# Head of a batch-norm matmul: one more small early read of x, wider early reads of w, eight small idle matmuls fewer

## The chip, the cores and the metric

The kernel runs on one core of one Trainium2 chip. The metric is the device time of one execution in microseconds (us). One execution was also recorded by the hardware profiler; its times are counted from the start of the span, that is from the first recorded instruction.

## The reference

`x` has 16 x 512 rows of 1024 values, `weight` (called w below) is 1024 x 768, both float32. Taken as one matrix, x has 8192 rows.

```
y = np.matmul(x, weight)
mean = np.mean(y, axis=(0, 1), keepdims=True)
var = np.var(y, axis=(0, 1), keepdims=True)
y_norm = (y - mean) / np.sqrt(var + eps)
return (gamma * y_norm + beta).astype(np.float32)
```

The mean and the variance of a column go over all 8192 rows, so nothing of a column can be written out before the whole column has been multiplied.

## The kernel before

**Tiling.** The rows of x are worked off in 16 chunks of 512 rows (`CH`). The 768 columns are six blocks of 128. In the first stage PE multiplies as x arrives: `rows_unit` (matmuls of line 493) makes column blocks 0 and 1 with rows on the partitions, and `col_unit` (matmuls of line 558) makes the other blocks with columns on the partitions, for the first chunks while x still arrives, for the others in later passes over x, which stays in SBUF. ACT and DVE take the results out of PSUM and collect sums; in the later stages the results are normalised, turned and stored. The last column block has an end of its own.

**Loading.** All loads of x and w are issued by POOL's queue and turn float32 into bf16 on the way. `load_x` (line 392) issues four transfers for each stretch of rows, one for each quarter of the 1024 columns. `load_w` (line 383) issues four transfers, one for each quarter `i` of w's 1024 rows. A quarter of w has four blocks of 64 rows, numbered by `jw`; two neighbouring rows are one 1536-value run on a partition. The first entries of the list of loads are

```
order = [("x", 0), ("w", 0, 2), ("x", 1), ("w", 2, 4)]
```

that is: x's first 256 rows (called x0 here), the blocks jw = 0 and 1 of every quarter (w's first pair), x's next 256 rows (x1), the blocks jw = 2 and 3 (w's second pair). Each is four transfers. A queue has eight completion slots, so a ninth transfer waits for the first one's landing, and so on.

**Turning x.** DVE transposes x's loaded rows into `xT_sb` (lines 414 and 421), for the first chunk in two halves per 256 rows.

**Order of work.** Tasks with a cost, dependencies and a due time go to a planner (`arrange`), which fixes one order of instructions per engine; `seq` chains the instructions of an engine in this order. The code around the change, the instructions ahead of the planner's first task, is written out by hand and is not planned.

**The head.** While the first loads are under way, three things happen that compute nothing of the result:

- `wake` (lines 574 and 577) runs idle matmuls on a cleared tile: `WAKE` = 8 with 512 float32 columns (each takes two passes in the profile), then `SMALL` = 16 small ones with 128 bf16 columns.
- `touched` (lines 342 to 345) is a small tile that nobody reads. SP issues four transfers into it, one for each quarter of w. Each reads a single 4-byte value out of every second row of block jw = 0, 32 values.
- a second call of `wake` (`FILL` = 1, one large idle matmul, two passes) stands between the first chunk's two halves.

After the first `wake`, PE's order is: eight matmuls of line 493 and sixteen of line 558 on x0 and w's first pair, the filling idle matmul, the same 24 matmuls on x1 and w's first pair, then the first chunk's matmuls with w's second pair.

Of the kernel before, what the change touches and what calls it, by code (L numbers as in the profile page):

```python
# [227 lines left out]
def kernel(  # L228
# [9 lines left out]
    nc = tc.nc  # L238
    f32 = mybir.dt.float32
# [8 lines left out]
    P = 128  # L248
# [5 lines left out]
    QR = 256  # L254
    QPC = CH // QR
    JW = KQ // 64
    PIECES = ((0,QR),(QR,QR))
    WAKE = 8
    FILL = 1
    SMALL = 16  # L260
    TOUCH = 1
    EARLY = 4
    SHORT = 2
# [16 lines left out]
    x_flat = x.flatten_outer_dims()  # L280
    out_flat = out.flatten_outer_dims()

    singles = ctx.enter_context(tc.tile_pool(name="singles", bufs=1))
# [7 lines left out]
    def seq(bi):  # L291

        ins = bi.ins
        prev = last.get(ins.engine)
        if prev is not None:
            tc.add_manual_dep(
                ins, prev,
                mybir.DependencyInfo(mybir.DependencyClass.NoSync, mybir.DependencyReason.DATA),
                reason="order",
            )  # L300
        last[ins.engine] = ins.name
        return bi
# [36 lines left out]
    warm = singles.tile([P, 1], f32)  # L339

    seq(nc.scalar.activation(warm, eps_sb, AF.Sqrt))
    touched = singles.tile([P, TOUCH], f32)
    first_rows = weight.rearrange("(i jw c e) n -> i jw c (e n)", i=4, jw=JW, e=2)
    for i in range(4):
        seq(nc.sync.dma_start(touched[32 * i:32 * i + 32], first_rows[i, 0, :, 0:TOUCH]))


    tasks, turns = [], {}
# [83 lines left out]
    t = 1.0  # L432
    affine = None
    for kind, n, *n1 in order:
# [21 lines left out]
        for i in range(rows // QR):  # L456
            c, q = divmod(m0 // QR + i, QPC)
# [9 lines left out]
        if rows % QR:  # L467
            t0 = rows // QR * QR // 32
            m1 = m0 + 32 * t0
            c, q = divmod(m1 // QR, QPC)  # L470
# [99 lines left out]
    def wake(count, slot):  # L570
        def emit(eng):
# [3 lines left out]
            small = idle_sb[:, 0:P // 2].bitcast(bf16)  # L575
            for _ in range(SMALL if count == WAKE else 0):
                seq(nc.tensor.matmul(idle_ps[:, 0:P], small, small, start=True, stop=True))
# [361 lines left out]
    k = 0  # L939
# [330 lines left out]
    for c, r0, rows in ends:  # L1270
        due = E + 2.0 + 0.6 * c
        n = max(rows // CH, 1)
# [70 lines left out]
```

## Time and profile before

| | |
|---|---|
| median of 3 runs | 207.59 us (207.12 to 207.87) |
| the profiled execution's own time | 207.45 us |
| its span, first to last instruction | 205.6 us |
| PE busy | 190.8 us, 93% of the span |
| DVE busy | 157.4 us, 77% |
| ACT busy | 139.9 us, 68% |
| POOL busy | 129.3 us, 63% |
| HBM read and written | 36.71 MB and 25.17 MB |

The 1.85 us between the profiled execution's time and its span lie ahead of the first and behind the last recorded instruction. A row of the timeline or of the chain gives the start and the length in us, then the engine, the line and the tiles; `x8` says that eight instructions are merged into it. "issue" in the chain is time in which an engine waits for nothing that the profile shows. In a table by windows, PEclk is the granted TensorE clock as a share of full speed, "DMA share" the packets' time as a share of the time of 16 DMA engines (above 1 where packets overlap), and GB/s what was moved, counted in bytes as written.

### The profile page before, as it was taken

The page shows a single profiled execution, that of the slowest core. Times are in us where ns is not written, and L with a number is a line of the kernel's source. Part 1 is how long each engine was busy: PE and PEld are TensorE (multiplying, and loading weights), DVE is VectorE, ACT ScalarE, POOL GpSimd, SP SyncE. Part 2 cuts the span into 40 slices and gives each one's busy share as a digit, 9 for nine tenths or more (in the row PEclk, how much of TensorE's full clock was granted, in tenths as well). Part 3 has the DMA queues.
Part 4 walks back from the last instruction along what each step waited for, and adds up shares of the span by engine and source line. Part 5 has one row for each costly group of instructions (what it writes and reads, how often), then busy time and mean ns, then how long its engine had stood idle before and what let it go on. Part 6 is the DMA issues. An engine that isn't in the chain of part 4 may idle for free.

```text
span 205.6 us, 3501 instructions
## 1 busy us (share of the span) xinstructions
PE 190.8 (93%) x1211; PEld 118.0 (57%) x1226; DVE 157.4 (77%) x239; ACT 139.9 (68%) x248; POOL 129.3 (63%) x143
## 2 busy tenths in 40 slices
PE   7999999999999999999999999999999999996900
PEld 3467565656588888777865444444444445553900
DVE  4202979989999999969989998888999648947900
ACT  2000461468989999998879777997376776875960
POOL 7766964787399979997304998599945440440000
PEclk9999999999999999999999999999999999999695
DMA  5999999999999999999696898999999999999898
GB/s 60 151 200 198 194 196 196 199 195 196 190 193 196 197 196 196 196 197 195 101 143 205 312 338 286 260 354 312 318 323 217 324 311 324 270 344 346 247 347 254
DMA packets 98433, 48.73 MB, mean 237 GB/s; under 512 B 24176, under 2 KB 97904, under 8 KB 98416
## 3 DMA queue, kind: packets, MB, share of 16 engines
q0 software_dynamic: 34624, 18.36, 65.2%
q1 hardware_dynamic: 63792, 30.16, 53.2%
q8 instruction: 9, 0.15, 0.3%
q14 instruction: 8, 0.07, 0.1%
HBM read 36.71 MB, written 25.17 MB: 301 GB/s over the span
## 4 chain that ended last, share of the span: by engine, by line
PE 86%; DMA 3%; ACT 3%; POOL 2%; issue 1%; DVE 1%; ACTq 0%; POOLq 0%
PE y_ps L558 53%; PE y_ps L493 24%; PE y_ps L797 4%; DMA w_sb<-in_weight_dram 3%; ACT o_sb L1292 3%; PE o_ps L1027 2%; POOL ring L392 1%; PE a_ps L886 1%; PE y_ps L736 1%; POOL w_sb L383 1%; PE o_ps L1057 0%; ACTq L1338 0%; PE idle_ps L574 0%; PE tot_ps L854 0%; DVE fin L743 0%
## 5 line engine op out<-in xcount | busy, mean ns | idle before, releaser
L558 PEld LDWEIGHTS <-w_sb 128*128 128x128 bf16 x520 | 50.4, 97 | 56.9
L558 PE MATMUL y_ps<-x_pl,w_sb 128*128 128x512 bf16 x256 | 60.5, 379 | 0.3
L392 POOL DMA_DIRECT2D ring<-in_x_dram x76 | 47.5, 629 | 14.2 <-DVE xT_sb L414 5.0
L558 PE MATMUL y_ps<-xT_sb,w_sb 128*128 128x512 bf16 (+1 forms) x249 | 55.0, 370 | 0.4
L493 PE MATMUL y_ps<-w_sb,xT_sb 128*128 128x256 bf16 x448 | 50.4, 273 | 0.6 <-DMA w_sb<-in_weight_dram 0.5
L493 PEld LDWEIGHTS <-xT_sb 128*128 128x128 bf16 x448 | 43.6, 98 | 8.0 <-issue 1.0
L421 DVE STREAM_TRANSPOSE xT_sb<-ring 128x1024 f32<-128x1024 f32 (+1 forms) x29 | 31.2, 1112 | 14.1 <-DMA ring<-in_x_dram 13.9
L694 DVE BATCH_NORM_STATS2 stats<-y_ps 128x6 f32<-128x512 f32 x46 | 30.8, 687 | 12.0 <-PE y_ps L558 11.8
L698 ACT CAST y_sb<-y_ps 128x512 bf16<-128x512 f32 x51 | 29.4, 590 | 13.3 <-DVE stats L694 11.3
L925 POOL TENSOR_TENSOR ring<-ring,sum 128x1024 f32<-128x1024 f32 (+1 forms) x11 | 23.8, 2192 | 14.6 <-DVE ring L920 14.6
L642 ACT ACTIVATE sq_sb<-y_ps 128x512 f32<-128x512 f32 x28 | 16.3, 610 | 17.9 <-PE y_ps L493 17.7
L649 POOL TENSOR_TENSOR sum<-sum,sq_sb 128x512 f32<-128x512 f32 x20 | 25.6, 1280 | 3.5 <-ACT sq_sb L642 2.7
L530 ACT COPY x_pl<-xT_sb 128x1024 bf16<-128x1024 bf16 x24 | 24.4, 1057 | 1.7 <-DVE xT_sb L421 1.7
L645 DVE TENSOR_TENSOR sum<-y_ps,sum 128x512 f32<-128x512 f32 x28 | 18.9, 675 | 6.3 <-ACT sq_sb L642 5.3
L655 ACT CAST y_sb<-y_ps 128x512 bf16<-128x512 f32 x28 | 16.1, 598 | 7.9 <-DVE sum L645 7.7
L530 POOL COPY x_pl<-xT_sb 128x1024 bf16<-128x1024 bf16 x15 | 16.4, 1128 | 7.7 <-DVE x_pl L530 4.9
L920 DVE TENSOR_TENSOR ring<-y_sb,a_ps 128x1024 f32<-128x1024 bf16 (+1 forms) x16 | 16.7, 1080 | 0.8 <-DMA out_dram<-ring 0.8
L1192 ACT CAST ring<-ring 128x1024 f32<-128x1024 bf16 x15 | 15.7, 1049 | 1.6 <-DMA ring<-y_sb 1.6
L1027 PE MATMUL o_ps<-ident,y_sb 128*128 128x128 bf16 x104 | 14.5, 248 | 2.2 <-DVE y_sb L1279 2.0
L1138 POOL TENSOR_TENSOR ring<-ring,sum 128x1024 f32<-128x1024 f32 x4 | 9.7, 2414 | 10.9 <-DVE ring L1134 10.9
L414 DVE STREAM_TRANSPOSE xT_sb<-ring 128x2048 bf16<-128x2048 bf16 x6 | 13.5, 2289 | 0.3 <-DMA ring<-in_x_dram 0.2
L574 PE MATMUL idle_ps<-idle_sb 128*128 128x512 f32 x18 | 10.7, 749 | 1.5 <-DVE idle_sb L314 1.5
(97 smaller groups left out, 155.1 us busy)
## 6 DMA issues: line engine op xcount, KB each, us to landing
out_dram<-ring SPq DMA_DIRECT2D x38, 512.0 KB, 3.8
ring<-in_x_dram POOLq DMA_DIRECT2D x52, 256.0 KB, 8.8
out_dram<-o_sb SPq DMA_DIRECT2D x6, 512.0 KB, 4.4
ring<-in_x_dram POOLq DMA_DIRECT2D x16, 128.0 KB, 6.0
w_sb<-in_weight_dram POOLq DMA_DIRECT2D x8, 192.0 KB, 6.2
out_dram<-ring SPq DMA_DIRECT2D x4, 256.0 KB, 3.1
ring<-in_x_dram POOLq DMA_DIRECT2D x4, 192.0 KB, 8.0
out_dram<-o_sb SPq DMA_DIRECT2D x3, 256.0 KB, 2.5
```

Of the source, the lines that this page charges most:

```text
L392: bi = seq(nc.gpsimd.dma_start(x_bf[32 * i:32 * i + 32], src[:, :, KQ * i:KQ * (i + 1)]))
L421: seq(nc.vector.transpose(dst, src[:, :, jw0:jw1]))
L493: seq(nc.tensor.matmul(y_ps[:, s], x_of(c, jw, e, t * P, (t + 1) * P), w_sb[:, jw, e, 0:NA], start=(s == 0 and jw == 0 and e == 0), stop=( ...
L530: seq(nc.scalar.copy(dst, pairs) if eng == "ACT" else ENG[eng].tensor_copy(dst, pairs))
L558: seq(nc.tensor.matmul(y_ps, w_sb[:, jw, e, nt * P:(nt + 1) * P], moving(c, jw, e, q0 * QR, q1 * QR, parted), start=(jw == 0 and e == 0 an ...
L645: seq(nc.vector.tensor_add(sum1, slot.tile[:, 0:n], sum1))
L649: seq(ENG[eng].tensor_add(acc, acc, state["sq"][:, 0:n]))
L694: seq(nc.vector.bn_stats(dst, slot.tile))
L698: seq(nc.scalar.copy(y(nt, c), slot.tile))
L920: seq(nc.vector.tensor_mul(slot.o, y_row[c].y[:, s0:s1], aff[0][:, None, :].to_broadcast([P, n, NA])))
L925: seq(ENG[eng].tensor_add(slot.o, slot.o, row[:, None, :].to_broadcast([P, n, NA])))
L1027: seq(nc.tensor.transpose(dst, src, ident))
```

## The change

Three edits, all at the head. The number of small idle matmuls goes from 16 to 8. SP issues one more small transfer, ahead of the others: one 4-byte value of each of x's first 256 rows. The four transfers on w read twice as many values, from blocks jw = 0 and jw = 1 instead of jw = 0 alone.

```
-    SMALL = 16
+    SMALL = 8
...
-    touched = singles.tile([P, TOUCH], f32)
-    first_rows = weight.rearrange("(i jw c e) n -> i jw c (e n)", i=4, jw=JW, e=2)
+    touched = singles.tile([P, 4, TOUCH], f32)
+    first_x = x_flat[0:QR].rearrange("(t p) k -> p t k", p=P)
+    seq(nc.sync.dma_start(touched[:, 2:4], first_x[:, :, 0:TOUCH]))
+    first_rows = weight.rearrange("(i jw c e) n -> i c jw (e n)", i=4, jw=JW, e=2)
     for i in range(4):
-        seq(nc.sync.dma_start(touched[32 * i:32 * i + 32], first_rows[i, 0, :, 0:TOUCH]))
+        seq(nc.sync.dma_start(touched[32 * i:32 * i + 32, 0:2], first_rows[i, :, 0:2, 0:TOUCH]))
```

The order of instructions on the other engines stays. PE has 16 rows fewer (eight matmuls and their weight loads), SP has one transfer more, ahead of the four.

## Prediction

> **What bounds the kernel now.** I read the chain that ended last first, because the change is all at the head and the chain tells whether the head reaches the end.
>
> ```profile
> PE 86%; DMA 3%; ACT 3%; POOL 2%; issue 1%; DVE 1%; ACTq 0%; POOLq 0%
> ```
>
> Then the same chain in order of time, its first pieces:
>
> ```profile
> 1.29 2.44 POOL ring L392 x4
> 3.74 1.21 POOL w_sb L383 x3
> 4.95 0.36 issue
> 5.31 7.09 DMA w_sb<-in_weight_dram
> 12.40 0.14 issue
> 12.53 1.03 PE y_ps L493 x8
> 13.57 1.81 PE y_ps L558 x16
> 15.38 0.86 PE idle_ps L574 x2
> 16.24 0.87 PE y_ps L493 x8
> 17.11 1.81 PE y_ps L558 x16
> 18.93 0.07 issue
> ```
>
> The only DMA in the chain is the fourth transfer of w's first pair, issued at 5.31 and landed at 12.40. From 12.53 to 187.96 the chain holds nothing but PE and issue pieces of about 0.05. So PE begins when w's first pair has landed, and whatever that landing gains is kept to the end, unless a later arrival takes its place. Next the timeline around that point, to see what PE does before it and what follows close behind:
>
> ```profile
> 10.96 1.06 PE L577 MATMUL idle_ps<-idle_sb 128*128 128x128 bf16 x16
> ...
> 12.53 1.03 PE L493 MATMUL y_ps<-w_sb,xT_sb 128*128 128x256 bf16 x8 [0.51 <-DMA w_sb<-in_weight_dram]
> ...
> 15.24 1.30 DVE L421 STREAM_TRANSPOSE xT_sb<-ring 128x512 f32<-128x512 f32 x2 [5.16 <-DMA ring<-in_x_dram]
> ```
>
> The idle matmuls end at 10.96 + 1.06 = 12.02, and PE then stands for 0.51 us. Last, the table by windows: how fast do the first transfers run?
>
> ```profile
> 3.50:4.50 1.00, 1.00 (x3) 0.48 (x2) 0.00 (x0) 0.00 (x0) 1.00 (x3) 1.00 1.21 149
> 4.50:5.50 1.00, 1.00 (x2) 0.39 (x2) 0.00 (x0) 0.00 (x0) 1.00 (x3) 1.00 1.19 150
> 5.50:6.50 1.00, 1.00 (x2) 0.34 (x1) 0.00 (x0) 0.00 (x0) 1.00 (x3) 1.00 1.43 125
> 6.50:7.50 1.00, 1.00 (x3) 0.38 (x2) 0.00 (x0) 0.30 (x1) 0.89 (x3) 1.00 0.92 100
> 7.50:8.50 1.00, 1.00 (x4) 0.49 (x3) 0.00 (x0) 0.00 (x0) 0.57 (x1) 1.00 0.92 136
> 8.50:9.50 1.00, 1.00 (x4) 0.46 (x3) 0.72 (x2) 0.00 (x0) 0.57 (x2) 1.00 1.11 212
> ```
>
> The last column is GB/s. From 8.5 to 18.5 the ten windows of 1 us give 212, 206, 194, 185, 193, 211, 221, 206, 207 and 182, mean 202. The five from 3.5 to 8.5 fall short of that by 1 - 149/202 and so on: 0.26 + 0.26 + 0.38 + 0.50 + 0.33 = **1.73 us of stream time lost**, 0.52 of it while only x0 flows, 1.21 where x0 ends and w begins. The same kinds of transfers for x1 and w's second pair, from 12 on, show no such dip.
>
> **The change part by part.**
>
> *Eight small idle matmuls fewer.* Sixteen start within 15/16 of 1.06 - 0.22 = 0.84 us (0.219 is one's duration), 0.056 apart, so eight fewer end 8 x 0.056 = 0.45 earlier, at 11.57. By themselves they bring nothing: PE then waits 0.96 instead of 0.51 for the same landing. They only set how early PE can take an earlier landing: 12.53 - 11.60 = 0.93 us is the most the change can gain in this execution.
>
> Does the longer gap cost the clock? The trace has two rows: the 0.51 gap left the granted clock at 1.00, and the 2.03 us at the tail (PE ends at 187.96 and resumes at 189.99) were followed by a clock of 0.50 in 192 to 194. A gap of 0.96 is nearer to 0.51, so I take nothing; the other end is a stretch at half speed like that tail's (0.50 over at least 2 us: 1 us of PE work lost; with 0.72 over 190 to 192 about 1.6). The Trainium skill, "TensorE: Matmul & The Clock Gate", section on the HAM clock gate, wants a whole idle window of about 3.4 us before the clock halves. The tail's row contradicts it, since 2.03 us were enough there; by the rule the gap would cost nothing even if w came 1 us late, by the row it might.
>
> *The wider touches.* What they may bring is a stream without the dip. Bounds: nothing, if the dip is not cured by reading the rows beforehand, and 1.73 us, if all of it is. Before, half of w's first pair is touched and nothing of x0; after, all of both. For it speaks that the dip has two parts, one on x0, untouched, and the deeper one where w's first pair begins, half untouched. Against it speaks that x1 and the second pair were never touched and run at 202 all the same. I take half, 0.87.
>
> The Trainium skill, "DMA: Bandwidth & Descriptors", section "Anatomy of one DMA", speaks against the change: a transfer costs a constant 2.0 us or so plus its bytes over a rate, with no term for a first read. By it nothing is gained, and the sum stays at 207.45 plus the price of the touches. The trace's windows from 3.5 to 8.5 do not follow a constant rate, so something is missing in it; whether it is a first read, no row says.
>
> *What the touches cost.* The touch row of before:
>
> ```profile
> L345 SPq DMA_DIRECT2D touched<-in_weight_dram x4: 397/412/423, 0.7 to 2.1; - x4
> ...
> DMA to landing us min/median/max: 1.5/2.0/2.7
> ```
>
> One more of them ahead pushes w's four by about 0.43 us on SP (the 128-partition loads of gamma take 0.434), where nothing else is queued until 48 us. The last would land at about 2.1 + 0.43 + 2.7 = 5.2, still ahead of w's first packets (w's four are issued from 3.74 and follow x0's). On the DMA engines the four touches are 192 packets, 48 each (32 values and 16 more); the DMA view for 2.5 to 5.5 counts 96 of them, 3.3% of 16 engines for 3 us, that is 16.5 ns each. After, x's touch has 272 packets, issued at 0.74, which mostly pass before x0's first data at about 2.8 (bandwidth 58 GB/s in 2.5 to 3.5), and w's have 80 each, three of them beside x0: 240 instead of 96. Cheap end: 144 x 16.5 ns / 16 = 0.15 us. Dear end: each takes the slot of a 512-byte packet of x (193 GB/s in 12.5 to 13.5 is 377 packets a us), and x's touch falls in too: (144 + 272) / 377 = 1.1 us. I take 0.2, near the measured 16.5 ns.
>
> *Sum.* Stream earlier by 0.87 - 0.2 = 0.67 us. PE is free at 11.57, so the first matmul moves from 12.53 to about 11.86. What is late next: x1's first half must be transposed by PE's 16.24. DVE's two pieces of 0.65 begin at 15.24, so the first is ready at 15.89, 0.35 early. Then w's second pair: POOL, which waits for its fourth landing, goes on at 19.15, and at the first pair it went on 0.28 after the landing (12.68 against 12.40), so it lands at 18.87, only 0.06 ahead of PE at 18.93. So PE's gain is the least of 0.93, 0.67 + 0.35 and 0.67 + 0.06: the stream must be earlier as a whole, not only its first piece. I take **0.7 us**. After 19 the loads of x are ahead of PE. 207.45 - 0.7 = 206.75 for the profiled execution; the median shown is 0.14 above it, so **206.9**, 0.33% less than 207.59.
>
> **The rivals.**
>
> *The dip stays.* Something of the first microseconds other than first reads slows the stream. The never-touched x1 and second pair, at full rate, speak for it, and so does the dip itself, which goes on until 8.5 with w's block jw = 0 already touched. PE waits 0.96 instead of 0.51, gain 0, less the 0.15 of the touches: 207.4 to 207.8 by the median.
>
> *The touches crowd out x0.* At 2.8 to 4.5 their 4-byte packets take turns with x0's on every DMA engine, x0 and so w land later, and PE, which stands already at 11.57, hands all of it on. Price 0.4 (144/377) to 1.1, with nothing cured: 208.0 to 208.7. It decides from the point where what they take exceeds what they cure, so at 0.4 us if less than a quarter of the 1.73 is cured; at the dear end the gap becomes 0.96 + 1.1 = 2.06, as long as the tail's, and the clock's 1 to 1.6 us could come on top. Against it: the touches in the trace took 16.5 ns each, and x0 at 4.5 to 5.5, when they are over, is no faster (150) than beside them (149).
>
> *The change does what it says but w's second pair does not follow*: then PE wins 0.06 to 0.3 at first and waits at 18.9: 207.3 to 207.5.
>
> **How the numbers follow.** Forecast 0.48; dip stays 0.27; crowding 0.18; second pair late 0.07. A measurement of this kernel can tell about 0.3%, 0.62 us, from no change. Of the forecast's cases (gain 0.4 to 0.95) I put 0.41 beyond 0.62 and 0.07 short of it; of the crowding 0.14 beyond and 0.04 short. Faster 0.41; within 0.07 + 0.27 + 0.04 + 0.07 = 0.45; slower 0.14. The range goes from the cap, 207.59 - 0.93 = 206.66, less 0.2 for the scatter of the runs, 206.45, to 208.15, which takes in the cheaper half of the crowding and leaves its dear end and the clock out, about 0.13. The forecast's own range is 206.6 to 207.2.
>
> **What would show it.** Right: GB/s above 180 in the windows from 3.5 to 8.5; w's fourth landing near 11.7; PE's line 493 at 11.6 to 12.0; then at about 18.3 the matmuls on the second pair, with no wait at either. If the dip stays: 100 to 136 GB/s at 5.5 to 8.5 and a wait of 0.96 ahead of line 493. If they crowd: less than 149 at 3.5 to 4.5 and that wait above 1.3. I am wrong if PE's first matmul moves and the end does not move with it.

## The result, and the profile after

The change makes the kernel **slower**: 208.21 us median of 22 runs (207.54 to 208.84) against 207.59 us of before in the same number (206.99 to 208.15); ratio 1.0027, 95% interval 1.0016 to 1.0038. The profiled execution took 208.22 us, with a span of 206.4.

The lines that answer to those of before, in the same order. The shares of the chain that ended last:

```profile
PE 79%; DMA 9%; ACT 3%; POOL 2%; DVE 1%; issue 1%; ACTq 0%; DVEq 0%; POOLq 0%
```

DMA has 9% instead of 3%: the chain runs through transfers three times now. Its first pieces:

```profile
1.30 2.44 POOL ring L394 x4
3.73 1.56 POOL w_sb L385 x3
5.30 7.10 DMA w_sb<-in_weight_dram
12.40 0.28 issue
12.69 6.18 DMA w_sb<-in_weight_dram
18.87 0.28 issue
19.16 6.00 DMA ring<-in_x_dram
25.16 0.03 issue
25.18 0.05 DVEq L423
25.23 0.05 issue
25.28 1.25 DVE xT_sb L423
26.54 0.05 issue
26.58 1.92 PE y_ps L495 x16
```

w's fourth landing is at 12.40, as before to the hundredth. The second pair's is at 18.87, where the prediction had worked it out for before. New is the piece behind it: a transfer of x's fourth 256 rows, issued at 19.16, lands at 25.16, and DVE's transposition and then PE wait for it. The timeline of after:

```profile
10.02 0.61 PE L579 MATMUL idle_ps<-idle_sb 128*128 128x128 bf16 x8
...
12.54 1.03 PE L495 MATMUL y_ps<-w_sb,xT_sb 128*128 128x256 bf16 x8 [1.91 <-DMA w_sb<-in_weight_dram]
...
25.28 1.25 DVE L423 STREAM_TRANSPOSE xT_sb<-ring 128x1024 f32<-128x1024 f32 x1 [0.95 <-DMA ring<-in_x_dram]
```

PE's first matmul is at 12.54 (12.53 before). It waits 1.91 us for it, longer than the 0.96 expected, because in this execution the clock was granted in full earlier, at 4.67 instead of 6.56 us, and the idle matmuls ended sooner. The last line is one part of the loss: before, the same transposition stood at 24.42 with no wait for a transfer in front of it. It is 0.86 us later; PE, which had 0.39 in hand there, begins the sixteen matmuls at 26.58, and all that PE does after that is late by 0.47 (its main work ends at 188.43 instead of 187.96). The line of before:

```profile
24.42 1.25 DVE L421 STREAM_TRANSPOSE xT_sb<-ring 128x1024 f32<-128x1024 f32 x1
```

That is not all of the 0.77 us between these two executions. By the trace's records the last store lands at 205.01 instead of 204.66, 0.35 later, but from this landing to the end of the span there are 1.35 us instead of 0.93. "The end of the program", below, shows what these 0.42 us are. Last the windows:

```profile
2.50:3.50 1.00, 1.00 (x3) 0.48 (x2) 0.58 (x4) 0.00 (x0) 1.00 (x3) 1.00 0.54 20
3.50:4.50 1.00, 1.00 (x3) 0.48 (x2) 0.00 (x0) 0.00 (x0) 1.00 (x3) 1.00 1.35 145
4.50:5.50 1.00, 1.00 (x3) 0.43 (x3) 0.00 (x0) 0.00 (x0) 1.00 (x3) 1.00 1.52 162
5.50:6.50 1.00, 1.00 (x3) 0.38 (x2) 0.00 (x0) 0.00 (x0) 1.00 (x3) 1.00 1.19 140
6.50:7.50 1.00, 1.00 (x4) 0.43 (x3) 0.00 (x0) 0.30 (x1) 0.91 (x3) 1.00 1.06 164
7.50:8.50 1.00, 1.00 (x4) 0.52 (x3) 0.00 (x0) 0.00 (x0) 0.58 (x1) 1.00 1.02 180
```

The dip is partly filled: against 202 GB/s, the five windows from 3.5 on lose 1.09 us where they lost 1.73. But x0 begins later, 20 GB/s at 2.5 to 3.5 instead of 58, which takes back 0.19 of the 0.64. So the stream as a mean gained 0.45 us. The landing gained nothing. The trace's records of single packets and landings say why. w's first pair is 256 packets; they end at 9.26 in the mean, 9.67 before, but the last one at 12.07, 12.08 before. A transfer is spread over 16 DMA engines, its landing is the last engine's, and the engines run apart. Their lags, set in the first 9 us, then stay as they are, transfer after transfer, up to 23 us:

```
landing of one transfer of x, us      first engine   last but one   last
before                                21.73          22.85          22.92
after                                 21.46          22.71          22.90
after, a later transfer               24.35          25.60          26.50
before, a later transfer              24.65          25.57          25.61
```

Between the two rows of after the last engine's lag behind the last but one grew from 0.19 to 0.90 us. A transfer of 16 KB on the queue that the profile calls "instruction" began there at 22.75 and took 0.96 us. In before it ran at 22.11 for 0.98 us, and by the landings the engine that fell back was the one most ahead: no landing came later for it.

### The profile page after: what moved, and what is told of

Same layout as the page of the kernel before. It is cut to its first block, busy times and chain, and to the rows that moved or that the text cites. A ratio compares the mean times of both kernels' runs of the same rounds, so it can differ in the third digit from the quotient of the medians.

```text
span 206.4 us, 3501 instructions
## 1 busy us (share of the span) xinstructions
PE 190.7 (92%) x1218; PEld 117.2 (57%) x1218; DVE 157.9 (77%) x239; ACT 139.2 (67%) x248; POOL 129.1 (63%) x143
## 4 chain that ended last, share of the span: by engine, by line
PE 79%; DMA 9%; ACT 3%; POOL 2%; DVE 1%; issue 1%; ACTq 0%; DVEq 0%; POOLq 0%
PE y_ps L560 50%; PE y_ps L495 21%; DMA w_sb<-in_weight_dram 6%; PE y_ps L799 4%; ACT o_sb L1294 3%; DMA ring<-in_x_dram 3%; PE o_ps L1029 2%; POOL ring L394 1%; PE a_ps L888 1%; PE y_ps L738 1%; POOL w_sb L385 1%; DVE xT_sb L423 1%; PE o_ps L1059 0%; ACTq L1340 0%; PE tot_ps L856 0%
## 5 line engine op out<-in xcount | busy, mean ns | idle before, releaser
L560 PE MATMUL y_ps<-x_pl,w_sb 128*128 128x512 bf16 x264 | 61.3, 379 | 0.0
L560 PE MATMUL y_ps<-xT_sb,w_sb 128*128 128x512 bf16 (+1 forms) x256 | 55.7, 370 | 0.0
L576 PE MATMUL idle_ps<-idle_sb 128*128 128x512 f32 x18 | 9.7, 692 | 1.5 <-DVE idle_sb L314 1.5
```

The lines of the kernel that those rows point to most:

```text
L560: seq(nc.tensor.matmul(y_ps, w_sb[:, jw, e, nt * P:(nt + 1) * P], moving(c, jw, e, q0 * QR, q1 * QR, parted), start=(jw == 0 and e == 0 an ...
```

## The experiments

Ratios are to before, with their 95% interval; "first matmul" and "transposition" (DVE's of x's fourth 256 rows) are from the one profiled execution of each kernel.

**Which edit?** Four kernels take the two sorts of edits apart.

e1, fewer idle matmuls alone:
```
-    SMALL = 16
+    SMALL = 8
```


> Before with 8 small idle matmuls instead of 16, touches as before. In the profile of the change w's first pair landed at 12.40 as before, so PE waited 1.91 us; later the fourth stretch of x landed 0.86 us late behind a 16 KB transfer on the instruction queue, which began at 22.75 instead of 22.11. Theory 'rows': taking 16 rows out of PE's program moves that transfer onto a DMA engine that is last: +0.6 us here, 1.003. Theory 'skew': the touches change which DMA engine is last: no change here, 1.000 (within 0.1%). Theory 'gap': the longer gap at the head lets the clock fall in some executions: +0.3 to +0.6 us, with executions up to 1.7 us longer.

**1.0003** (0.9991 to 1.0016): nothing, as theory "skew" said. But its profiled execution (208.07 us) shows the same late transposition with before's touches:

```profile
25.02 1.25 DVE L421 STREAM_TRANSPOSE xT_sb<-ring 128x1024 f32<-128x1024 f32 x1 [0.94 <-DMA ring<-in_x_dram]
```

So the collision is no property of the change; before can meet it too.

e2, the diff of the touches alone, `SMALL = 16`:

> The change's five touches with 16 small idle matmuls as before. Theory 'rows': 1.000, PE's program is that of before. Theory 'skew': +0.6 us, 1.003, and x's fourth stretch again late by 0.9 us. Theory 'gap': 1.000 or 0.1 us less, the gap is that of before.

**1.0038** (1.0024 to 1.0053): the whole loss is in the touches. Profiled 208.71 us, first matmul 12.63, and again:

```profile
25.32 1.25 DVE L423 STREAM_TRANSPOSE xT_sb<-ring 128x1024 f32<-128x1024 f32 x1 [0.90 <-DMA ring<-in_x_dram]
```

e3 and e4, before's touches and other idle matmuls:
```
e3:  SMALL = 8, matmul(idle_ps[:, 0:2 * P], small, idle_sb[:, 0:P].bitcast(bf16))
e4:  SMALL = 8, and a second loop of 8: matmul(idle_ps[:, 0:8], small, small[:, 0:8])
```


> Before with 8 small idle matmuls of 256 columns instead of 16 of 128: 16 rows fewer on PE, the same time (8 x 0.107 against 16 x 0.056 us). Theory 'rows': 1.003, as for the 8 of 128 columns. Theory 'gap': 1.000, the gap is that of before. Theory 'skew': 1.000.

> Before with 8 small idle matmuls of 128 columns and 8 of 8 columns: as many rows on PE as before, about 0.2 to 0.4 us less time. Theory 'rows': 1.000. Theory 'gap': +0.1 to +0.5 us, between before and the 8 alone. Theory 'skew': 1.000.

1.0001 (0.9989 to 1.0013) and 0.9998 (0.9989 to 1.0007). "Rows" and "gap" are both out: neither the number of PE's instructions nor the gap matters here.

**Which touch?**

e5 and e6, with `SMALL = 16`:
```
e5:  the four wider touches of w, no touch of x
e6:  the touch of x ahead of before's four touches of w
```


> The four wider touches of w without the touch of x, 16 small idle matmuls as before. Shown so far: the five touches alone make the kernel 1.0038 slower, the fewer idle matmuls do nothing; and in all six profiles the executions in which the 16 KB instruction transfer at 22 to 23 us falls on the DMA engine that is last are the slow ones (207.45, 207.25 and 207.84 us without, 208.22, 208.07 and 208.71 with). Theory 'stalls moved': the wider w touches take the long first packets of w away (over 1.3 us each), and without them the engine that carries the instruction transfer is last more often: 1.002 to 1.004 here. Theory 'crowding': the price is the 272 packets of x's touch ahead of x0: 1.000 here, up to 1.001.

> The touch of x's first 256 rows ahead of the four touches of w as before, 16 small idle matmuls. Theory 'stalls moved': w's long first packets stay, 1.000 to 1.001. Theory 'crowding': x0 begins 0.1 to 0.3 us later and its landing with it: 1.002 to 1.004.

e5: 0.9997 (0.9984 to 1.0009). e6: **1.0031** (1.0020 to 1.0041). "Stalls moved" falls, since the wider touches alone cost nothing; the loss is the touch of x. In e6 the profiled execution (208.28 us) is late at the head, not at the transposition:

```profile
12.87 1.03 PE L495 MATMUL y_ps<-w_sb,xT_sb 128*128 128x256 bf16 x8 [1.13 <-DMA w_sb<-in_weight_dram]
...
24.75 1.25 DVE L423 STREAM_TRANSPOSE xT_sb<-ring 128x1024 f32<-128x1024 f32 x1
```

e7 and e8 were to move the 16 KB transfer away, with the change's and with before's touches:
```
-    WAKE = 8
+    WAKE = 9
-    SMALL = 8      (e8: 16)
+    SMALL = 0
```


> The change's five touches, and at the head 9 large idle matmuls and no small one instead of 8 and 8: the idle matmuls end within 0.5 us of before's, with 28 instructions fewer than before on PE. If the 16 KB transfer at 22 to 23 us is PE's program, it is asked for 28 instructions later, and with matmuls of 0.22 us per pair it should begin some 2 to 3 us later, when x's fourth stretch is through. Theory 'instruction transfer on the last engine': the 0.86 us is gone, 207.6 to 207.8, 1.000 to 1.001. If the touches cost in another way: 1.003 to 1.004 as with the touches alone. If the transfer does not move, the run tells nothing of this.

> Before's four touches with 9 large idle matmuls and no small one. Theory 'instruction transfer on the last engine': the executions of before that are hit by it (its slower third, up to 208.1) go, so the median falls by 0.1 to 0.3 us, 0.999, and the longest are below 207.9. Otherwise 1.000.

1.0034 (1.0021 to 1.0048) and 1.0005 (0.9994 to 1.0016). The transfer did not move (22.98 and 22.22 us), so they tell nothing of its part, as the expectation allowed.

**What of the fifth transfer costs?** All with before's touches of w behind it and `SMALL = 16`, but for e9.
```
e9:   e5 with SMALL = 8
e10:  first_x = weight[3 * QR:4 * QR].rearrange("(t p) k -> p t k", p=P)
e11:  first_x = x_flat[0:2 * QR]..., touched[:, 2:6]
e12:  dma_start(touched[0:1, 2:3], first_x[0:1, 0:1, 0:TOUCH])
```


> The wider touches of w with 8 small idle matmuls, no touch of x: two of the change's three edits. In the profile with the wider touches alone the first matmul began at 12.22 right behind the idle matmuls (12.14), so w had landed by then and PE was the later one. Theory 'wider w touches help the head': 0.1 to 0.4 us less than before, 0.998 to 0.9995. Theory 'the landing does not move': 1.000.

> Before's four touches, and ahead of them a fifth of the same size as x's touch, 256 values on 128 partitions, but out of w's last 256 rows. The touch of x alone gave 1.0031. Theory 'packets' (272 small packets ahead of x0 cost, whatever they read): 1.002 to 1.004. Theory 'x read early' (that it is x's rows that are read matters): 1.000.

> The touch of x with x's first 512 rows, 512 values and 528 packets instead of 272. Theory 'packets': twice the price, 1.005 to 1.007, and x0's landing another 0.3 us later. Theory 'a fifth transfer on SP pushes w's four touches': 1.003, as with 256 values.

> The touch of x cut to one single value, ahead of the four touches of w as before. Theory 'packets': 1.000, at most 17 packets more. Theory 'a fifth transfer on SP pushes w's four touches by 0.4 us into x0': 1.002 to 1.004.

e10: 1.0028 (1.0015 to 1.0041). It reads w, not x, and costs the same: that x's rows are read is neither use nor harm. e11: 1.0018 (1.0006 to 1.0030), e12: 1.0016 (1.0003 to 1.0030). Neither theory's numbers: twice the packets do not cost twice, and a single value, two packets by the trace, costs already.

e9: **0.9985** (0.9972 to 0.9998), 207.41 us, the lowest of all. Among eighteen kernels one interval that ends at 0.9998 may be chance. Profiled 207.08 us:

```profile
5.32 6.47 DMA w_sb<-in_weight_dram
```

w's fourth transfer lands at 11.79 and the first matmul is at 11.93, just what the prediction had hoped of the whole change (11.86). And this execution was hit by the 16 KB transfer on its last engine as well; as its engines lay only 0.81 apart (after: 1.44), the transposition came at 24.57.

**Place or packets?** e13 to e16:
```
e13:  e6 with the touch of x behind w's four
e14:  e6 with nc.scalar.dma_start for the touch of x, ahead of ACT's first activation
e15:  no touch at all
e16:  the change with the touch of x behind w's four
```


> The touch of x's first 256 rows behind w's four touches instead of ahead of them, 16 small idle matmuls. Theory 'push' (w's four come 0.43 us later): they are back at their place, 1.000, at most 1.001. Theory 'packets' (272 more beside x0, now right in x0's stream): 1.003 or more.

> The touch of x issued by ACT's queue at its start, ahead of the table load, so that SP's four touches of w stay where they were. Theory 'push': 1.000. Theory 'packets': 1.002 to 1.004.

> No small early transfer at all, 16 small idle matmuls. Theory 'push': w's touches are worth something by coming early, so without them w lands later: 1.002 to 1.005, with w's first packets long. If touches are of no use: 0.999 to 1.000, and the price of a fifth one is its packets.

> All three edits of the change, but with x's touch behind w's four. The wider w touches with 8 small idle matmuls alone gave 0.9985. Theory 'push': x's touch costs little here, 0.9985 to 1.000. Theory 'packets': 1.002 to 1.004, as the change itself.

e13: 1.0021 (1.0007 to 1.0036). e14: 1.0017 (1.0002 to 1.0032). e15: 1.0012 (0.9995 to 1.0028), unclear. e16: **0.9993** (0.9977 to 1.0009). e16 is the change but for the order of its five transfers, and its interval does not overlap with that of the change (1.0016 to 1.0038). But its median, 207.83, lies above that of before in the same rounds, 207.65, so the two estimates point opposite ways; that the place of x's touch matters with the wider touches is not shown. With the narrow touches the place makes no clear difference (e13 against e6). So neither theory holds for both.

e17 and e18 bring w's values earlier, in fewer transfers:
```
e17:  dma_start(touched, first_rows[:, 0, :, 0:TOUCH])                         SMALL = 16
e18:  for jw in range(2): dma_start(touched[:, jw:jw + 1], first_rows[:, :, jw, 0:TOUCH])   SMALL = 8
```


> Before's 128 values of w in one transfer instead of four, so that all are read by 0.4 us of SP time instead of 1.6, 16 small idle matmuls. Theory 'number and place of the transfers on SP' (a fifth ahead costs 0.0016 to 0.0031): 0.998 to 0.9995, w's first pair lands 0.1 to 0.4 us earlier. If only the packets beside x0 count: 0.9995 to 1.0005, as the packets that remain are 128 and 16.

> The 256 values of w's first pair in two transfers instead of four, with 8 small idle matmuls, no touch of x. The same values in four transfers gave 0.9985. Theory 'number and place': 0.997 to 0.9985. Theory 'packets': 0.998 to 0.999, as with four.

e17: 1.0014 (0.9994 to 1.0035), e18: 0.9998 (0.9989 to 1.0008). "Number and place" expected a gain and there is none: earlier is not better as such.

**The end of the program.** Seven profiles have a fifth transfer ahead of w's four (after, e2, e6, e7, e10, e11, e12), five have the four of before (before, e1, e3, e4, e8):

```
means, us                                      with a fifth ahead (7)    the four of before (5)
first matmul                                   12.71 (12.54 to 12.89)    12.45 (12.29 to 12.62)
16 KB transfer on the last engine              4 of 7                    1 of 5
end of PE's main work                          188.44                    188.09
from there to the last store's landing         16.76                     16.79
from that landing to the end of the span       1.35 (1.35 to 1.36)       0.92 (0.92 to 0.93)
```

Among the other eight the 16 KB transfer fell on the last engine twice (e9, e14).

The last row is the same within 0.01 us in every profile of a group, and no chain shows it, because a chain ends with the last working instruction. When the program ends, SP waits for the eight completion slots of its queue, one after the other, in the order of the slots' numbers. In after a wait whose slot is done still takes 0.06 us. SP's transfers take the slots in turn, in before and after from the lowest number on. In before SP issues 88 transfers, eleven times eight, so the last store has the slot that is waited for last. In after there are 89, and the last store has the slot that is waited for first: when it lands, SP still has to walk through the other seven. SP's instructions of the closing line, from just before the last store's landing on, in before and in after:

```profile
L1338 SPq EVENT_SEMAPHORE  x3: 17/17/28, 204.7 to 205.5; - x3
...
L1340 SPq EVENT_SEMAPHORE  x10: 17/28/28, 205.0 to 206.3; - x10
```

Seven waits more, 0.42 us, whatever the fifth transfer reads, however much, and wherever it stands. All 20 profiles fit:

```
early transfers of SP                     kernels                           landing to end, us
four                                      before, e1, e3, e4, e5, e8, e9    0.92 to 0.93
five                                      after, e2, e6, e7, e10-13, e16    1.35 to 1.36
none, one, two                            e15, e17, e18                     1.16, 1.11, 1.05
four, and one of ACT                      e14                               1.36
```

The measured time holds this end in full: it is 1.85 to 1.89 us longer than the span in 19 of the 20 (1.78 in e14). With none, one or two early transfers the last store's slot has four, three or two others behind it. In e14 SP's turn begins at another number, and the last store's slot is waited for first as well. The time agrees: the medians of the ten kernels with 1.35 or 1.36 us lie 0.18 to 0.92 us above before's of the same rounds, 0.53 in the mean; those of the six others with four touches lie from 0.30 below to 0.12 above. For e15, e17 and e18 the end accounts for 0.24, 0.18 and 0.13 us, which lies within the interval of each.

What is left between the two groups is 0.35 us at the end of PE's main work. In all 20 profiles that end is the later of two times, the first matmul plus 175.43 us and the transposition plus 163.15 us, or up to 0.36 after it. So both late arrivals of the head reach the end.

## Why the prediction was wrong

*What bounds the kernel*: right. The first matmul waits for w's first pair, and what e9 gained at its landing (12.53 to 11.93) came out at the end (207.45 to 207.08), 0.37 of 0.60.

*Eight idle matmuls fewer bring nothing by themselves*: right, 1.0003 in e1. The clock stayed at 1.00 over the gap of 1.91 us too, so the cheaper end was the true one. The tail's row, on which the dearer end rested, does not repeat: the gap there is 2.04 or 2.05 us in all 20 profiles, and a clock of 0.50 followed within 4 us of its start in twelve of them, in the other eight not for 11 us.

*The failed step* is "Stream earlier by 0.87 - 0.2 = 0.67 us. PE is free at 11.57, so the first matmul moves from 12.53 to about 11.86." By the step's own count of GB/s the stream did come 0.64 us earlier, 0.45 with x0's later start. But I let a mean stand for a landing, and the first matmul stayed at 12.54. The first matmul needs the last of 16 engines, and that engine's work ended at 12.07 in place of 12.08. The rate in a window can rise while the engine that counts gains nothing; the sign that would have warned stood in the trace, in the spread of a single transfer's landings over the engines (1.2 us). That is why there is no gain; the next two points are why there is a loss.

*What is late next*: I looked at x1 and at w's second pair and wrote "After 19 the loads of x are ahead of PE". In before they were, with 0.39 us for x's fourth 256 rows. That reserve was not worked out, and it is smaller than the 0.96 us that a 16 KB transfer takes on one engine.

*The touches' price* was put at 0.15 to 1.1 us, by packets on the DMA engines at the head, and taken as 0.2. As a size that holds the loss; as a mechanism it does not: 528 packets cost no more than 272, and two packets half as much (e11, e6, e12). The fifth transfer was followed along SP only as far as w's four touches, "where nothing else is queued until 48 us"; for the end of the program the sum had no term, without a reason. There it costs 0.42 us, two thirds of the 0.62 between the medians.

*The crowding*: the time, 208.21, lies in its range of 208.0 to 208.7, and its signs, a wait above 1.3 and less than 149 GB/s at 3.5 to 4.5, were fulfilled (1.91 and 145). But the wait came from the earlier full clock, with the landing unmoved. What the touches do crowd out is x0's start: its first transfer is through on the first of the engines at 4.27 to 4.40 us in the seven kernels with a 128-partition transfer ahead of x0 (after, e2, e6, e7, e10, e11, e14) and at 4.03 to 4.19 in the thirteen others. w's fourth landing does not follow that: 12.24 to 12.75 in the seven, 11.79 to 12.80 in the others.

*The dip as a first read*: not confirmed. w's packets over 1 us, six in before, are gone in after, but also without any touch (e15), where x0's take more time instead; and with the touches of w as wide as in after there are one in e5 and two in e9.

What stays open is the other third. In the seven profiles with a fifth transfer ahead the first matmul is 0.26 us later in the mean, and the 16 KB transfer meets the last engine more often; that this meeting makes the transposition late is shown by the waits in those executions. Why the last engine should be later with a fifth transfer, and whether the medians lose by it, is not shown: the profiles are few, and the two runs that were to move the 16 KB transfer did not.

## What to carry to other kernels

Read the landing of a transfer, not the rate of the stream: it is the last of 16 DMA engines that lands it, and work that makes only the others faster gains nothing. When a change is several small edits, time each alone; here two cost nothing, and the third, a single transfer, cost more than they could bring. When a small transfer has the same price whatever it reads, look behind the last store too: the chain that ended last does not go there, and one transfer more on a queue changes which of the closing waits comes last. And for each later arrival work out the reserve before calling it covered, in the size of the disturbances that the trace shows (1 us on one engine).

## What the runs showed of the hardware

The lags between the 16 engines, once there, hardly changed from 11.5 to 22.9 us, over more than a dozen transfers: first and last engine lay 1.16 to 1.23 us apart in before, 1.38 to 1.50 in after. The first 16 KB transfer on the instruction queue took 0.94 to 0.98 us in the 20 profiles; in after the engine that it met lay 1.19 us behind the last but one at that transfer and 0.86 to 0.95 at the next four, where it had lain 0.15 to 0.20 behind. It came at 22.1 to 23.1 us in all 20 profiles, also with 28 PE instructions fewer ahead of it (e7 and e8). The second 16 KB transfer does move with PE's program: it came at 40.8 us in before, at 42.0 in after, and at 44.7 in e7 and e8.

At the end of the program SP's waits for completion slots that are already done took 0.06 us each, so the end took 0.92 us from the last store's landing with that store's slot waited for last, and 1.35 with it waited for first.
